# A two-layer hybrid decoder on one core: the first latent pair's rotary turn and key product move behind five steps of the next query projection

## The chip, the cores and the metric

One core of one Trainium2 chip runs the whole program in one launch. The metric is the device time of one execution in microseconds (us). PE is TensorE, with its weight loads apart (PEld); DVE is VectorE, ACT is ScalarE, POOL is GpSimd, SP is SyncE, whose queue issues the DMAs.

## The reference, cut to what matters

512 tokens of width 1024 go through two layers. Each begins with a mixer of three groups of heads: six latent heads (MLA) with a decoupled rotary key, six differential heads, four block-sparse heads (MoBA). Then come a cross-attention and an MLP.

```python
proj = n @ w_in                        # c_q 256, c_kv 128, k_r 32, dq dk dv 384 each, mq mk mv 256 each
qh  = to_heads(rmsnorm(c_q, q_norm) @ w_uq, 64 + 32)
kvh = to_heads(rmsnorm(c_kv, kv_norm) @ w_ukv, 64 + 64)
q_a = concatenate([qh[..., :64], apply_rope(qh[..., 64:], pos)])
k_a = concatenate([kvh[..., :64], broadcast(apply_rope(k_r, pos))])   # one rotary key for all six heads
o_a = causal_attention(q_a, k_a, kvh[..., 64:])
lam = exp(sum(lq1 * lk1)) - exp(sum(lq2 * lk2)) + lam_init
o_b = rmsnorm(diff_attention(dq, dk, dv, lam), sub_norm) * (1 - lam_init)
o_c = moba_attention(mq, mk, mv)
h = h + concatenate([o_a, o_b, o_c]) @ w_out
```

The output is the (1, 512, 1024) float32 trunk after both layers and a final norm.

## The kernel before, in words

**Precision.** Every float32 operand is kept as two parts, a high part (cast on ACT) and the rest (a subtraction on DVE or POOL), side by side in one tile. A product is three matmuls, high by high, high by low, low by high (`mm3`). `split` (L135, its casts L139, its subtractions L141) makes the two parts of an activation; for the kinds in `pool_kinds` ("mq", "kr", "q", "cq", "lat") the subtraction is on POOL, else on DVE. `halve` (L153) does the same for a weight block: ACT L156, then L161, in the mixer on POOL for the even blocks or as `vector_full` sets it. The subtraction of a score operand must end before the scores that read it.

**Work of the mixer** (L751). Eight pairs of heads, m0 to m2 (latent), d0 to d2 (differential), o0 and o1 (MoBA), have two kinds of work. *Units* (`head_units`): for one head and one block of 128 queries the scores on PE (128 to 512 columns), the mask and maximum on DVE (L637), the exponential on ACT (L639), the reciprocal and scaling on DVE (L707, L708; the second block's scaling on POOL), two units later the transposes of the probabilities (L279, evictions L671, L672), and per head a product with the values (`mix`). *Steps* (`Filler`, L55): the projections that make the pairs' queries, keys and values, in the order `fill_order` (L1434): kv, cq, tok, m0, d0, m1, d1, o0, m2, d2, o1, mem, cross. A 128x512 projection is eight steps (`proj_steps`, L288), each with three matmuls of 128x512 (a *step* below), one tick, and at its first and fifth step a weight block of 128x512. `weights` (L196) fetches two blocks ahead of the one that it hands out, so a step issues a load on SP's queue (L150, from `w_in` or `w_mla`) and its halving too.

The pipeline (L728) starts a unit, then draws steps worth `fill_time` from the filler, then finishes an older unit. The steps are thus what PE does while a unit's softmax is under way; their number in a layer is fixed. Before a pair's first unit, `drain` (L75) runs all steps up to that pair. `after(n, call)` (L307) hangs a call on a count of ticks (`tick`, L311). Matmuls of `mm3` are emitted with `hold=False`: the scheduler may move them, so the order on PE isn't quite that of the code.

**Around the change.** `tok` projects d0's and d1's values and the 32 columns of the rotary key. Its eviction is followed by `rotate` (L828): six small DVE operations (L834 to L836) turn the key by the positions' angles, a copy (L837) doubles it. `rotate` hangs `turn` (L840) on `chain_k` ticks: four transposes on PE into a "t" bank (L279), a copy on ACT (L846), a split of kind "kr" (ACT, then POOL, 64x512) into the first of four key tiles, and three DMAs on SP (L852) that copy it into the others. `mla_steps` for m0 makes the values of the pair (twelve matmuls of 128x128), the two queries (two 128x512 products of six matmuls, each multiplied by the rotary table, L889, and split on ACT and POOL, kind "mq"), then at L895 waits for the keys by ticking, and makes the key product (three matmuls of 128x512, L897 to L900), which is split on ACT and DVE into the lower halves of two key tiles. The scores of m0's first head need its query, the first key tile's both halves and nothing else. In layer 0 the lambda of the differential heads is computed beside the first units: a load (L475) and eight small DVE operations (L480, L481), then L487 and L488.

PSUM banks: three "mm" (projections), three "s" (scores, `mix`), two "t" (transposes).

Of the kernel before, what the change touches and what calls it, by code (L numbers as in the profile page):

```python
# [48 lines left out]
class Filler:  # L49
# [17 lines left out]
    def run(self, time):  # L67

        busy = False
        while self.todo and self.todo[0][2] in self.over and time > 0:  # L70
            time -= self.step()
            busy = True
        return busy
# [27 lines left out]
class Trunk:  # L101
# [649 lines left out]
    def mixer(self, l):  # L751
# [4 lines left out]
        fill = Filler()  # L756
# [101 lines left out]
            self.cq = yield from latent_steps([a["w_in"][l, 1], a["w_in"][l, 2]],  # L858
                                              self.gains["g_q"][:, 2 * l:2 * l + 2], 256)

        def mla_steps(p, got):
            def ready(there):
                while not there():
                    self.tick()

            ready(lambda: None not in self.ckv)
            (ckv,), cq = self.ckv, self.cq
            ws = [self.weights(a["w_mla"][l, p, :, :4 * P]), self.weights(a["w_mla"][l, p, :, 4 * P:])]

            def wb(j):  # L870
                js = slice(j % 4 * P, (j % 4 + 1) * P)
                return ws[j // 4][:, 0, js], ws[j // 4][:, 1, js]


            ps = self.psum("mm" if p else "t")
            for i in range(NQ):
                isl = slice(i * P, (i + 1) * P)
                self.mm3(ps[:, isl], (ckv[:, 0, isl], ckv[:, 1, isl]), wb(5), True, True)
            got["v"] = self.evict_values(ps)
            self.tick(2)  # L880
            yield 1300
            ready(lambda: None not in cq)
            got["q"] = []
            for e in range(2):
                ps = self.psum("mm")
                for j in range(2):
                    self.mm3(ps, wb(2 * e + j), (cq[j][:, 0, :], cq[j][:, 1, :]), j == 0, j == 1)
                t = self.tmp()
                nc.vector.tensor_tensor(t, ps, self.tab_q, ALU.mult)  # L889
                q = self.pair("B")  # L890
                self.split(q[:, 0, :], q[:, 1, :], t, kind="mq")
                got["q"].append(q)
                self.tick(2)
                yield 1280
            ready(lambda: self.keys)  # L895

            ps = self.psum("mm")  # L897
            self.mm3(ps, wb(4), (ckv[:, 0, :], ckv[:, 1, :]), True, True)
            got["k"] = self.keys[2 * (p % 2):2 * (p % 2) + 2]
            for e, k in enumerate(got["k"]):  # L900
                self.split(k[0:64, 0, :], k[0:64, 1, :], ps[64 * e:64 * e + 64, :])
            self.tick()
            yield 640

        def mla_units(p, got):
            units = []
            oo = {}

            def o():
                if "o" not in oo:  # L910
                    oo["o"] = self.tmp()
                return oo["o"]

            def done():
                outs[p] = self.finish_pair(o())

            for e in range(2):
                def terms(e=e):
                    q, k = got["q"][e], got["k"][e]
                    return [(q[:, i, :], k[:, j, :]) for i, j in ((0, 0), (0, 1), (1, 0))]  # L920

                units += self.head_units([terms], lambda i: self.causal[:, S - (i + 1) * P:], 1.0,
                                         lambda: got["v"], e, o, None, done if e else None)
            return units
# [28 lines left out]
        def pair_steps(p, got):  # L953

            at = 3 + 2 * p if p < 2 else 1 + 3 * p
            if p < 3:
                yield from qk_steps(at, got, "q", p, 2, (0, 0, 1))
                yield from qk_steps(at + 1, got, "k", None, 2, (0, 1, 0))
            else:
                yield from qk_steps(at, got, "q", p, 1, (0, 1))  # L960
                yield from qk_steps(at + 1, got, "k", None, 1, (0, 0), (1, 1))
            if p < 2:
                return

            ps = yield from self.proj_steps(a["w_in"][l, at + 2], x)

            def evict():
                t = self.tmp()
                nc.vector.tensor_tensor(t, ps, self.hnorm.rows, ALU.mult)
                self.after(3, lambda: turn(t))  # L970

            def turn(t):
                vt = self.psum("t")
                for i in range(NQ):
                    self.transpose(vt[:, i * P:(i + 1) * P], t[:, i * P:(i + 1) * P])
                got["v"] = self.evict_values(vt)

            self.hnorm.then(evict)
# [78 lines left out]

        got = {n: {"moves": []} for n in "d0 d1 d2 m0 m1 m2 o0 o1".split()}
        self.keys = []
        steps = {"kv": kv_steps, "cq": cq_steps, "tok": token_steps}  # L1060
        steps["mem"] = lambda: self.memory_steps(l)
        steps["cross"] = lambda: self.cross_memory_steps(l)
        units = {}
        for p in range(3):
            steps[f"d{p}"] = lambda p=p: pair_steps(p, got[f"d{p}"])
            steps[f"m{p}"] = lambda p=p: mla_steps(p, got[f"m{p}"])
            units[f"d{p}"], units[f"m{p}"] = pair_units(p, got[f"d{p}"]), mla_units(p, got[f"m{p}"])
        for p in range(2):
            steps[f"o{p}"] = lambda p=p: pair_steps(3 + p, got[f"o{p}"])
            units[f"o{p}"] = pair_units(3 + p, got[f"o{p}"])  # L1070
        for n in self.fill_order.split():
            fill.add(n, steps[n](), "m0" if n == "m2" else None)
        seq = []
        order = self.fill_order.split()
        for n in self.unit_order.split():
# [352 lines left out]
    def run(self):  # L1428
        nc = self.nc
        self.bufs = {"A": 8, "B": 21, "tmp": 11, "small": 40, "raw": 4, "w": 5, "pt": 2}  # L1430
        self.pbufs = {"mm": 3, "s": 3, "t": 2}
        self.ptags = {"o": "s"}

        self.fill_order = "kv cq tok m0 d0 m1 d1 o0 m2 d2 o1 mem cross"  # L1434
        self.unit_order = "m0 d0 m1 d1 o0 m2 d2 o1"
        self.fill_time = {1: 1870, 2: 1700}
        self.cross_fill_time = 4000
        self.mem_time = 300

        self.skew, self.tail_skew = 2, 2  # L1440

        self.wait_n, self.wait_l, self.wait_d = 8, 3, 3
        self.pow_d = 3
        self.chain_n, self.chain_l, self.chain_d, self.chain_k = 6, 12, 4, 2

        self.pool_kinds = ("mq", "kr", "q", "cq", "lat")
        self.vector_full = self.vector_all = False

        self.look, self.mlp_look = 2, 6
        self.plan = self.planned()  # L1450
        self.blocks = sum(1 for _ in self.planned())
        self.fetched = 2
        self.setup()
        g = self.gains
        self.sum_squares_start()
        self.hn = [self.norm_input(k, g["g_attn"][:, :KT], squares=False) for k in range(KT)]
        for k in range(KT):
            self.after(2 + k, lambda k=k: self.sum_squares_add(self.h[k], True))
        self.hnorm = Later()
        self.after(10, lambda: self.norm_of(self.hnorm, self.sq, NQ, 2))  # L1460
        self.setup_gains()
        self.after(12, self.setup_rotary)
        for n, part in enumerate(self.setup_distances()):
            self.after(24 + 2 * n, part)
        self.after(58, self.setup_lambda)
        self.memory_norm(34, 8)
        for l in range(L):
            gs = slice(l * KT, (l + 1) * KT)
            self.vector_full = True
            outs = self.mixer(l)  # L1470
            self.vector_full = False
            self.output(self.a["w_out"][l], outs, g["g_cross"][:, gs], (3, 0, 4, 1, 5, 2, 6, 7))
            outs = self.cross(l)
            parts = {n: [] for n in ("11", "21", "22", "t1", "t2", "t3", "t4", "y")}
            self.vector_all = True
            self.output(self.a["w_co"][l], outs, g["g_mlp"][:, gs], halves=parts)
            self.mlp(l, g["g_attn"][:, (l + 1) * KT:(l + 2) * KT] if l + 1 < L else None, parts)
            self.vector_all, self.look = False, 2
# [101 lines left out]
```

## Time and profile before

| | us |
|---|---|
| median of three runs | 1527.31 |
| the three runs | 1530.01, 1527.31, 1525.93 |
| the profiled execution, its own time | 1524.68 |
| its span | 1522.6 |
| PE busy | 1478.7 (97%) |
| DVE busy | 1048.5 (69%) |
| ACT busy | 854.1 (56%) |
| POOL busy | 362.9 (24%) |

The span is that of the instructions in the trace; the rest of the execution's time lies around them. The trace's mean TensorE clock is 0.995 of full speed. The times below are from the start of the span: layer 0's mixer has its units from about 62 to 274 us, layer 1's from about 812 to 1017 us.

### The profile page before, as it was taken

To read this page: it belongs to the slowest core of one execution; us is meant where nothing else is said; L and a number is where in the kernel's file an instruction comes from. 1 tells how busy PE (TensorE), PEld (TensorE's weight loads), DVE (VectorE), ACT (ScalarE), POOL (GpSimd) and SP (SyncE) were. 2 spreads that over 40 slices of the span, in tenths; PEclk is the share of its full clock that TensorE was granted. 3 is DMA by queue.
4 is the path that set the end of the run, shared out by engine and by line. 5 is a ranking of instruction groups with operands and counts; after the bars stand their busy time and mean duration, and the time that the engine had idled before them with its cause. 6 is when DMAs were issued, how large, how long until landed. Compare 5 with 4: busy or idle time off the path is not lost.

```text
span 1522.6 us, 24399 instructions
## 1 busy us (share of the span) xinstructions
PE 1478.7 (97%) x8648; PEld 1293.8 (85%) x8648; DVE 1048.5 (69%) x2316; ACT 854.1 (56%) x1823; POOL 362.9 (24%) x302
## 2 busy tenths in 40 slices
PE   7899999999999999999999999999999999999997
PEld 6778897888899899998887888888888989899887
DVE  7687887536699666676437788873378976677653
ACT  5576777535566544454446677764366654445441
POOL 2645374441000000000146446644400000000001
PEclk9999999999999999999999999999999999999999
DMA  4445543221223323223224535423202332333331
GB/s 154 125 107 140 153 133 110 81 93 49 88 72 125 108 92 100 98 103 97 97 75 122 154 101 158 114 90 96 98 30 76 110 120 92 103 98 103 111 98 56
DMA packets 90136, 157.22 MB, mean 103 GB/s; under 512 B 12064, under 2 KB 17056, under 8 KB 90016
## 3 DMA queue, kind: packets, MB, share of 16 engines
q1 hardware_dynamic: 89728, 155.63, 33.3%
q8 instruction: 68, 1.11, 0.3%
q14 instruction: 52, 0.43, 0.1%
q10 hardware_dynamic: 288, 0.05, 0.0%
HBM read 136.24 MB, written 2.10 MB: 91 GB/s over the span
## 4 chain that ended last, share of the span: by engine, by line
PE 74%; DVE 11%; ACT 5%; DMA 4%; issue 3%; POOL 2%; SPq 1%; POOLq 0%; DVEq 0%; ACTq 0%
PE mm L276 60%; PE s L276 11%; PE t L279 2%; DMA raw<-w 2%; ACT tmp L639 2%; DVE tmp L637 2%; DVE pt L672 1%; DVE tmp L712 1%; POOL w L161 1%; DVE tmp L260 1%; DVE B L141 1%; PE t L276 1%; ACT w L156 1%; DVE tmp L688 1%; DMA raw<-w_in 1%
## 5 line engine op out<-in xcount | busy, mean ns | idle before, releaser
L276 PE MATMUL mm<-B,w 128*128 128x512 f32 (+1 forms) x2490 | 574.3, 386 | 1.5 <-POOL B L141 1.4
L276 PEld LDWEIGHTS mm<-B,w 128*128 128x128 f32 x2490 | 453.2, 189 | 94.8 <-POOL B L141 2.8
L276 PE MATMUL mm<-A,w 128*128 128x512 f32 (+1 forms) x1920 | 384.7, 350 | 6.3 <-ACT A L143 5.9
L156 ACT CAST w<-raw 128x512 fp32r<-128x512 f32 (+1 forms) x372 | 224.7, 607 | 269.4 <-PE mm L276 209.0
L276 PEld LDWEIGHTS mm<-A,w 128*128 128x128 f32 x1920 | 310.1, 189 | 50.3 <-ACT A L143 5.9
L161 POOL TENSOR_TENSOR w<-raw,w 128x512 fp32r<-128x512 f32 (+2 forms) x180 | 226.7, 1267 | 218.9 <-ACT w L156 170.5
L409 POOL TENSOR_TENSOR tmp<-tmp,tmp 128x512 f32<-128x512 f32 (+1 forms) x25 | 30.1, 1206 | 655.3 <-ACT tmp L406 653.2
L161 DVE TENSOR_TENSOR w<-raw,w 128x512 fp32r<-128x512 f32 x192 | 134.7, 702 | 35.0 <-ACT w L156 34.7
L639 ACT ACTIVATE tmp<-tmp,small 128x384 f32<-128x384 f32 (+3 forms) x176 | 98.8, 562 | 60.2 <-DVE small L637 59.9
L1092 DVE TENSOR_TENSOR h<-mm,h 128x512 f32<-128x512 f32 x92 | 63.2, 687 | 67.9 <-PE mm L276 67.6
L276 PE MATMUL mm<-pt,B 128*128 128x256 f32 x768 | 102.9, 283 | 2.3 <-ACT tmp L1331 2.3
L139 ACT CAST B<-tmp 128x512 fp32r<-128x512 f32 (+2 forms) x156 | 91.9, 590 | 23.2 <-DVE tmp L688 5.9
L276 PEld LDWEIGHTS mm<-pt,B 128*128 128x128 f32 x768 | 95.8, 189 | 3.5 <-ACT tmp L1331 3.5
L260 DVE TENSOR_TENSOR tmp<-raw,raw 128x512 f32<-128x512 f32 x64 | 43.9, 686 | 66.1 <-DMA raw<-w 65.9
L263 ACT CAST B<-tmp 128x512 fp32r<-128x512 f32 x96 | 59.5, 620 | 51.2 <-DVE tmp L260 51.2
L279 PE MATMUL t<-ident,tmp 128*128 128x128 f32 (+1 forms) x444 | 75.0, 275 | 8.5 <-DVE tmp L837 3.2
L141 DVE TENSOR_TENSOR B<-tmp,B 128x512 fp32r<-128x512 f32 (+1 forms) x110 | 74.9, 681 | 12.1 <-ACT B L139 8.6
L279 PEld LDWEIGHTS t<-ident,tmp 128*128 128x128 f32 (+1 forms) x444 | 54.7, 141 | 24.2 <-issue 4.2
L141 POOL TENSOR_TENSOR B<-tmp,B 128x512 fp32r<-128x512 f32 (+1 forms) x46 | 61.9, 1353 | 48.2 <-ACT B L139 48.2
L276 PE MATMUL s<-pt,B 128*128 128x512 f32 (+3 forms) x352 | 71.3, 345 | 0.0
L338 POOL TENSOR_TENSOR small<-small,mhalf 128x4 f32<-128x4 f32 (+2 forms) x19 | 23.4, 1230 | 199.3 <-DVE small L372 174.5
L276 PE MATMUL mm<-w,A 128*128 128x512 f32 (+1 forms) x288 | 65.2, 365 | 3.6 <-DVE B L144 2.9
(195 smaller groups left out, 2115.1 us busy)
## 6 DMA issues: line engine op xcount, KB each, us to landing
raw<-w SPq DMA_DIRECT2D x256, 256.0 KB, 2.8
raw<-w_in SPq DMA_DIRECT2D x64, 256.0 KB, 3.2
st<-B SPq DMA_DIRECT2D x144, 64.0 KB, 2.0
raw<-w_ck SPq DMA_DIRECT2D x32, 256.0 KB, 3.0
raw<-w_cv SPq DMA_DIRECT2D x32, 256.0 KB, 2.7
raw<-w_out SPq DMA_DIRECT2D x32, 256.0 KB, 2.7
raw<-w_cq SPq DMA_DIRECT2D x32, 256.0 KB, 2.7
raw<-w_co SPq DMA_DIRECT2D x32, 256.0 KB, 2.6
```

The source lines that it names most:

```text
L139: nc.scalar.copy(hi, x)
L141: eng.tensor_tensor(lo, x, hi.bitcast(F32), ALU.subtract)
L156: self.nc.scalar.copy(w[:, 0, :], raw)
L161: eng.tensor_tensor(w[:, 1, :], raw, w[:, 0, :].bitcast(F32), ALU.subtract)
L260: nc.vector.tensor_tensor(got[name], x, y, op)
L263: nc.scalar.copy(w[:, 0, :], raw)
L276: self.in_order(self.nc.tensor.matmul(out, lhs, rhs, start=start, stop=stop, skip_group_check=open), hold)
L279: self.in_order(self.nc.tensor.transpose(out, x, self.ident))
L409: eng.tensor_tensor(s[:, :n], s[:, :n], self.sq[:, :n], ALU.add)
L637: nc.vector.tensor_tensor_reduce(out=t[:, :n], in0=s[:, :n], in1=bias, scale=-slope, scalar=TOP, op0=ALU.add, op1=ALU.min, accum_out=st[:, ...
L639: nc.scalar.activation(t[:, :n], t[:, :n], AF.Exp, bias=st[:, 0:1], scale=-1.0, accum_out=sums)
L1092: nc.vector.tensor_tensor(self.h[m], ps, self.h[m], ALU.add)
```

## The change

`chain_k` goes from 2 ticks to 11: the two of m0's values, two for each of its two queries, and five steps of the next entry of the fill order, d0, whose query projection is its first work. At L895 the loop that only ticked now draws steps of d0 until the rotary key is there. So in each layer the turn, its split and its DMAs, and m0's key product come after five of the eight steps of d0's query projection, which had come behind them. Those 15 matmuls are no longer there for the units later; the number of matmuls is the same.

```diff
-        def mla_steps(p, got):
+        def mla_steps(p, got, work):
...
-            ready(lambda: self.keys)
+
+            while not self.keys:
+                yield next(work["d0"])
...
+        work = {}
...
-            steps[f"m{p}"] = lambda p=p: mla_steps(p, got[f"m{p}"])
+            steps[f"m{p}"] = lambda p=p: mla_steps(p, got[f"m{p}"], work)
...
         for n in self.fill_order.split():
-            fill.add(n, steps[n](), "m0" if n == "m2" else None)
+            work[n] = steps[n]()
+            fill.add(n, work[n], "m0" if n == "m2" else None)
...
-        self.chain_n, self.chain_l, self.chain_d, self.chain_k = 6, 12, 4, 2
+        self.chain_n, self.chain_l, self.chain_d, self.chain_k = 6, 12, 4, 11
```

Lines of the changed kernel are two to four higher behind these places (L1156 becomes L1160, L932 becomes L934).

**PE, layer 0, from m0's last query product to its first scores**, before. `t_690` is the bank of the turn, `mm_730` m0's key product, `mm_750` d0's query projection, `s_740` the first scores.

```order
L279 MATMUL t_690<-ident,tmp_635 64x128 x4
L276 MATMUL mm_730<-B_572,w_613 128x512 x3
L276 MATMUL mm_750<-A_123,w_666 128x512 x3
L276 MATMUL mm_750<-A_126,w_666 128x512 x3
L276 MATMUL mm_750<-A_129,w_666 128x512 x3
L276 MATMUL mm_750<-A_132,w_666 128x512 x3
L276 MATMUL mm_750<-A_135,w_671 128x512 x3
L276 MATMUL mm_750<-A_138,w_671 128x512 x3
L276 MATMUL mm_750<-A_141,w_671 128x512 x3
L276 MATMUL mm_750<-A_144,w_671 128x512
L276 MATMUL s_740<-B_697,B_715 128x128 x3
```

The same place of the change (`t_745`, `mm_761`, `mm_714`, `s_771`):

```order
L276 MATMUL mm_714<-A_123,w_666 128x512 x3
L276 MATMUL mm_714<-A_126,w_666 128x512 x3
L276 MATMUL mm_714<-A_129,w_666 128x512 x3
L276 MATMUL mm_714<-A_132,w_666 128x512 x3
L276 MATMUL mm_714<-A_135,w_671 128x512 x3
L279 MATMUL t_745<-ident,tmp_635 64x128 x4
L276 MATMUL mm_761<-B_572,w_613 128x512 x3
L276 MATMUL mm_714<-A_138,w_671 128x512 x3
L276 MATMUL mm_714<-A_141,w_671 128x512 x2
L276 MATMUL s_771<-B_752,B_699 128x128
L276 MATMUL mm_714<-A_141,w_671 128x512
L276 MATMUL mm_714<-A_144,w_671 128x512 x2
```

Five steps stand ahead of the turn; of the eight, three are left behind the key product, partly between the first scores. Layer 1 reads the same.

**POOL, layer 0, the same place**, before. L161 halves a weight block, L141 of 128x512 is a query of m0, of 64x512 the rotary key.

```order
L161 TENSOR_TENSOR w_753<-raw_751,w_753 128x512
L161 TENSOR_TENSOR w_787<-raw_785,w_787 128x512
L141 TENSOR_TENSOR B_697<-tmp_695,B_697 64x512
L161 TENSOR_TENSOR w_824<-raw_822,w_824 128x512
L161 TENSOR_TENSOR w_905<-raw_903,w_905 128x256
L141 TENSOR_TENSOR B_715<-tmp_713,B_715 128x512
L141 TENSOR_TENSOR B_727<-tmp_725,B_727 128x512
```

And now:

```order
L161 TENSOR_TENSOR w_717<-raw_715,w_717 128x512
L161 TENSOR_TENSOR w_739<-raw_737,w_739 128x512
L141 TENSOR_TENSOR B_699<-tmp_697,B_699 128x512
L141 TENSOR_TENSOR B_711<-tmp_709,B_711 128x512
L161 TENSOR_TENSOR w_812<-raw_810,w_812 128x512
L141 TENSOR_TENSOR B_752<-tmp_750,B_752 64x512
L161 TENSOR_TENSOR w_871<-raw_869,w_871 128x256
```

The rotary key's split was ahead of the two queries' splits and comes behind both, and behind the next weight block (`w_812`), four operations of POOL in a row.

**DVE, layer 0, in m0's first units**, before. L480 and L481 are lambda's, `mm_750` is d0's query projection.

```order
L934 SCALAR_TENSOR_TENSOR tmp_814<-mm_750,qscale,rows_383 128x512
L672 TENSOR_TENSOR pt_857<-t_858,pt_857 128x128
L707 RECIPROCAL small_797<-small_796 128x1
L708 TENSOR_SCALAR tmp_802<-tmp_802,small_797 128x384
L672 TENSOR_TENSOR pt_857<-t_886,pt_857 128x256
L480 TENSOR_TENSOR small_832<-tmp_830 128x32
```

And now, from the last of lambda's eight small operations (`mm_809` is d0's key projection, `small_855` the third block's sum):

```order
L481 TENSOR_REDUCE small_821<-small_820 128x1
L637 ISA tmp_860,small_861<-s_856,causal 128x384
L637 ISA small_861 128x1
L487 TENSOR_TENSOR neg_lam<-small_822 128x1 x2
L488 TENSOR_SCALAR neg_lam<-neg_lam 128x1 x2
L707 RECIPROCAL small_855<-small_854 128x1
L637 ISA tmp_894,small_895<-s_890,causal 128x512
L637 ISA small_895 128x1
L708 TENSOR_SCALAR tmp_860<-tmp_860,small_855 128x384
L934 TENSOR_TENSOR tmp_906<-mm_809,rows_383 128x512
```

The eviction of d0's key projection (`tmp_906`) has come behind lambda's operations and the third block's scaling; the bank of `mm_809` is the one that PE needs for the second query product of m1.

## Rows read from the trace of the kernel before

**Rows 1.** The page, part 1: busy us (share of span), instructions.

```profile
PE 1478.7 (97%) x8648; PEld 1293.8 (85%) x8648; DVE 1048.5 (69%) x2316; ACT 854.1 (56%) x1823; POOL 362.9 (24%) x302
```

**Rows 2.** The waits of PE: engine, tile, line, releaser: us total, times, longest.

```profile
PE s L276 <- DVE tmp L688: 3.2, 6, 0.7
PE t L279 <- DVE tmp L837: 3.2, 2, 2.4
...
PE t L279 <- DVE tmp L708: 2.6, 1, 2.6
...
PE t L279 <- POOL tmp L708: 1.1, 1, 1.1
...
PE s L276 <- POOL B L141: 0.4, 2, 0.2
```

**Rows 3.** Timeline, PE, layer 0: start us, duration us, what, xcount [idle before, releaser].

```profile
53.30 2.12 PE L276 MATMUL mm<-B,w 128*128 128x512 f32 x8 [0.29 <-POOL B L141]
56.15 0.63 PE L279 MATMUL t<-ident,tmp 128*64 128x128 f32 x4 [0.73 <-DVE tmp L837]
...
57.31 5.17 PE L276 MATMUL mm<-A,w 128*128 128x512 f32 x22
62.33 0.33 PE L276 MATMUL s<-B,B 128*128 128x128 f32 x2
62.86 1.26 PE L276 MATMUL s<-B,B 128*128 128x128 f32 x7 [0.20 <-POOL B L141]
```

**Rows 4.** Timeline, PE, layer 1, the same place.

```profile
801.67 2.11 PE L276 MATMUL mm<-B,w 128*128 128x512 f32 x8 [0.28 <-POOL B L141]
806.22 0.63 PE L279 MATMUL t<-ident,tmp 128*64 128x128 f32 x4 [2.44 <-DVE tmp L837]
...
812.92 1.26 PE L276 MATMUL s<-B,B 128*128 128x128 f32 x7 [0.17 <-POOL B L141]
```

**Rows 5.** Timeline, POOL, layer 0, then layer 1.

```profile
56.20 1.29 POOL L161 TENSOR_TENSOR w<-raw,w 128x512 fp32r<-128x512 f32 x1 [1.70 <-ACT w L156]
...
808.25 1.29 POOL L141 TENSOR_TENSOR B<-tmp,B 64x512 fp32r<-64x512 f32 x1 [2.43 <-ACT B L139]
```

**Rows 6.** Timeline, DVE, layer 0, then layer 1: rotation, copy, query times table.

```profile
52.00 1.32 DVE L835 TENSOR_TENSOR tmp<-tmp,nsin 128x64 f32<-128x64 f32 x1
...
54.63 0.21 DVE L835 TENSOR_TENSOR tmp<-tmp,sin 128x64 f32<-128x64 f32 x1
...
805.93 0.23 DVE L837 COPY tmp<-tmp 128x128 f32<-128x128 f32 x1
806.08 1.28 DVE L889 TENSOR_TENSOR tmp<-mm,tab_q 128x512 f32<-128x512 f32 x2
```

**Rows 7.** Timeline, ACT, layer 0: the rotary key's first half.

```profile
57.43 0.62 ACT L139 CAST B<-tmp 64x512 fp32r<-64x512 f32 x1
```

**Rows 8.** Timeline, PE, layer 0 from 73 us, then layer 1.

```profile
73.35 1.45 PE L276 MATMUL mm<-w,B 128*128 128x128 f32 x12
77.38 0.63 PE L279 MATMUL t<-ident,tmp 128*128 128x128 f32 x4 [2.58 <-DVE tmp L708]
...
78.37 4.50 PE L276 MATMUL mm<-B,w 128*128 128x512 f32 x12
...
824.35 2.92 PE L276 MATMUL mm<-B,w 128*128 128x512 f32 x12
```

**Rows 9.** Windows, PE: us, PE busy (matmuls), granted clock, DMA share, GB/s.

```profile
78.00:81.00 3.00, 3.00 (x11) 0.56 0.23 53
...
807.00:809.00 2.00, 2.00 (x10) 1.00 0.33 110
```

**Rows 10.** Timeline, SP queue and DVE, layer 0: lambda's load and first product.

```profile
61.46 7.22 SPq L150 DMA_DIRECT2D raw<-w_in  x4
68.72 0.42 SPq L475 DMA_DIRECT2D tmp<-lam  x1
...
72.16 0.19 DVE L480 TENSOR_TENSOR small<-tmp 128x32 f32<-128x32 f32 x1 [1.50 <-DMA tmp<-lam]
```

## The prediction, made before the changed kernel ran

> **What bounds the kernel now.** I read the busy shares first, then the waits of PE, then the two places of the change in the timelines. PE is busy 1478.7 us, 97% of the span [rows 1], so what it idles, 43.9 us (the span of 1522.6 less that), is all that a change of order can win, and most of that isn't in reach. The waits [rows 2] show what is near the change: the turn's transposes wait for DVE's copy (L837) 3.2 us in two places, one in each layer; the first scores for POOL's split (L141) 0.4 us in two places; and in m0's units transposes wait once for POOL's scaling, 1.1 us, and once for DVE's scaling, 2.6 us. The last row of them, six waits of scores for DVE of 0.7 us at most, lies at the ends of the mixers.
>
> PE's timeline gives each its place. In layer 0 the last query product ends at 53.30 + 2.12 = 55.42, the turn waits 0.73 us, turn and key product take 56.15 to 57.31, and after the projection the scores wait 0.20 [rows 3]. In layer 1 the same waits are 2.44 and 0.17 [rows 4]. One matmul of 128x512 takes (62.33 - 57.31) / 22 = 0.228 us [rows 3]; this is the unit of all cover below.
>
> **What the profiled time is.** The sum is made against the profiled execution, 1524.68 us with 2.1 us outside its span; the median of the runs shown is 2.6 above it, and I put the sum on the median.
>
> **The change, part by part.** No matmul is added or taken away, and each moved step has its loads and halvings with it. Five steps, 15 matmuls or 3.4 us, go ahead of the turn in both layers, so there the copy is no longer waited for. What is late next is the rotary key's split on POOL. It now stands behind both queries' splits and one weight block; before, it stood ahead of them. PE sees it in the first scores.
>
> *Layer 1.* PE: 801.67 + 2.11 + 3.42 (five steps) + 1.16 (turn and key product) + 1.14 (five more matmuls ahead of the scores) = 809.50. POOL: the first query's product with its table can take the copy's place on DVE at 805.93 and lasts 0.64, half of 1.28 [rows 6]; its cast takes 0.62 [rows 7]; then come four operations of 1.29 each [rows 5], so the key is split at 805.93 + 0.64 + 0.62 + 5.16 = 812.35. Here the first score matmul needs only the key's high part, and it and three projection matmuls (0.8) fit in between. The new idle is 812.35 - 809.50 - 0.8 = 2.05, for 2.44 + 0.17 = 2.61 before [rows 4]: **-0.6**. Ends: -2.6 if POOL isn't late, +0.2 if nothing fits in between.
>
> *Layer 0.* PE is at the scores at 55.42 + 3.42 + 1.16 + 1.14 = 61.14. POOL is free of the weight block before at 56.20 + 1.29 = 57.49 [rows 5], and the same four operations end at 62.65. The first score matmul waits for the split here. Idle 1.5, for 0.73 + 0.20 before [rows 3]: **+0.6**. Ends: -0.9 and +1.2. The upper end is one more hold-up between DVE and POOL: the small rotation on DVE took 1.32 us where POOL worked beside it and 0.21 where not [rows 6], and an addition of two tiles on DVE (L1160) now stands beside those four operations.
> The Trainium skill, SBUF — State Buffer, section Who interferes with whom, says that a DVE instruction with two inputs in SBUF contends with a GpSimd instruction that reads SBUF, and whichever is first holds the port to its end. The two rotations agree, 1.32 against 0.21. By that rule the split would be later by up to an addition's length, about 0.65, and the sum 0.65 less negative; which engine is first there no row shows, so I leave it in the upper end.
>
> *Layer 0, m0's units.* The 1.1 us for POOL's scaling and the 2.6 us for DVE's [rows 2] are there because DVE's chain waits 1.50 us for lambda's load [rows 10]. After the second of these idles the clock is granted at 0.56 [rows 9], about half of 2.4 GHz, and 12 matmuls take 4.50 us for 2.92 in layer 1 [rows 8], 1.6 more. That is 5.3 in all, and it is this arrangement that the change breaks up. The key moves on SP come later, and two of the weight loads that stood behind them are ahead; lambda's load stood behind four loads in 7.22 us [rows 10], and so goes 2 x 1.8 = 3.6 earlier, at 65.1. It lands 72.16 - 68.72 = 3.4 later, at 68.5. Then DVE is no longer held by it but by the first block's transposes: 62.65, 22 matmuls (5.0), score products (about 1.4), transpose and evictions (about 0.75) give 69.8. From lambda to the scaling that PE waited for the chain took 77.38 - 72.16 = 5.2 [rows 8, 10], now to 75.0; and the eviction of d0's key projection, which now comes behind it, ends 0.64 later, 75.65. PE reaches the product that needs this bank at 62.65 + 11.7 = 74.35 (before, from 62.86 to 73.35 + 1.45 less the idle of 1.1 it had 10.8 of work; eight matmuls of 0.228 come in, a score product and two groups of transposes, some 0.9, go out). Idle 1.3, and 0.64 for one more eviction that the next bank waits for: 2.0 for 5.3. **-3.3**. That is under the 2.44 after which layer 1 kept its full clock [rows 4, 9], so I count no lost clock. Ends: -5.3 (no wait) and +0.6 (lambda lands as late as before; worked out below).
>
> *The ends of the mixers.* The steps moved ahead are missing later. By the order, PE has 71 projection matmuls between the transposes of the last three heads before and 58 now, in both layers: 13 x 0.228 = 3.0 us less cover, where DVE already makes PE wait 0.6 to 0.7 at a time [rows 2]. Output-projection matmuls fill in part. I take one to two more such waits, 1.0 a layer: **+2.0**. Ends: 0 and 2 x 15 x 0.228 = +6.8.
>
> *The middle units, the SP queue, the other keys.* Waits there are regrouped, none over 1.5: 0, ends -2 and +2. The three key moves are issued about 5 us later, but the first score that reads a copied key comes some 9 us after the first scores; if that cover went, it would be one landing, a case I give no share.
>
> Sum: -0.6 + 0.6 - 3.3 + 2.0 = **-1.3**, so 1523.4 against the profiled 1524.68 and 1526.0 on the median.
>
> **Rivals.**
> A, *the stalls just go*: POOL has time enough, lambda's and the bank's waits vanish, the ends have cover to spare. -2.6 - 0.9 - 5.3 = -8.8, 1518.5. For it: each of these waits lies next to a matmul that could fill it, and PE is the only bound. Against it: POOL's four operations in a row are longer than PE's work beside them in both layers.
>
> B, *the cover runs out at the ends, slower*: the last heads lack the moved matmuls one for one. +6.8 in place of +2.0 gives a sum of +3.5, 1530.8, and with one fall of the clock like that of [rows 8], 1.6, 1532.4. It decides once the ends cost more than the 3.3 that the rest gives back. For it: the number of steps is fixed, and these heads wait for DVE already. Against: 0.7 at most in each such wait, with no lost clock.
>
> C, *lambda's load comes no earlier*: SP is held by the key moves or the weight buffers. Then the chain ends at 77.38 + 0.64 = 78.0, PE idles 3.65 there, 0.64 behind it, and loses the clock's 1.6: 5.9 for 5.3. The sum is +2.6, 1529.9. For it: SP issues in order, and the moves still wait for POOL, later than before. Against: two of the four loads do stand ahead now.
>
> That the change doesn't do what it says is out: the five steps stand ahead of the turn in the order of both layers.
>
> **How the numbers follow.** 0.3% is 4.6 us, about what a measurement of this kernel can tell from no change. My forecast has 0.50, A 0.23, B 0.14, C 0.13. Faster (below 1522.7) is A and 0.04 of the forecast, 0.27; slower (above 1531.9) is 0.12 of B and 0.01 of C, 0.13; between them 0.60. The range goes from 1520.0, which takes in much of the way to A, to 1531.5, which takes in C and the lower half of B; about 0.1 is left out at either end.
>
> **What would show it.** Right: no wait of the transposes for L837 in either layer; scores that wait for POOL's L141 about 1.5 and 2.0 us; a wait of a projection for DVE's L934 near 75 us, and full clock behind it; lambda's first product no longer waiting for its load; at most 1 us more idle a layer at 255 to 274 and at 998 to 1017. Wrong: the POOL wait under 0.5 in both (A), DVE still waiting for lambda past 71 us (C), several waits on L688 of 1 us and more at the ends (B).

## The result, and the profile after

The change made the kernel slower: 1551.65 us in the median of four runs (1549.22 to 1558.66) against 1526.62 (1525.0 to 1530.01), a ratio of 1.0168 with a 95% interval of 1.0141 to 1.0194. That is 25 us, where the forecast was no change and the range ended at 1531.5.

The profiled execution took 1558.66, 7 above its median; its span is 1556.9. Of that, 2.2 us lie ahead of anything that the change moves: m0's last query product ends at 57.67 us for 55.42 [rows 3]. The page, part 1:

```profile
PE 1500.9 (96%) x8648; PEld 1306.6 (84%) x8648; DVE 1065.0 (68%) x2316; ACT 853.6 (55%) x1823; POOL 359.6 (23%) x302
```

No matmul was added, yet PE is busy 22.2 us longer than in [rows 1]; it idles 56.0 us (1556.9 less 1500.9), 12.1 more than before. So a third of the 34 us of span is idle time, and two thirds are the same matmuls taking longer. Most of these two thirds is the clock: its mean is 0.984 here and 0.995 before, 1.6% of the one span and 0.5% of the other, which makes some 17 us (an estimate). That share belongs to this execution. The other three of the changed kernel have a mean clock of 0.989 to 0.991, and by the same working 6 to 9 us are clock, of the 25 to 28 by which their spans are longer than that of before. The waits of PE (columns as in [rows 2]; a line behind the change has a number two higher, so L1036 is L1034 of before):

```profile
PE t L279 <- DVE tmp L1036: 6.6, 2, 3.5
...
PE t L276 <- ACT tmp L1024: 4.1, 3, 1.9
...
PE mm L276 <- DVE tmp L934: 3.1, 1, 3.1
...
PE mm L276 <- ACT w L156: 2.6, 1, 2.6
...
PE mm L276 <- POOL w L161: 2.3, 5, 0.6
...
PE s L276 <- POOL B L141: 1.8, 2, 1.0
...
PE s L276 <- DVE tmp L688: 1.0, 3, 0.4
```

The waits that the prediction began with are gone: no transpose waits for L837, nor for L708, and the waits for L688 are 1.0 us where they were 3.2 [rows 2]. What came is new: L1036 and L1024, the norm chain of a differential pair (squares on ACT, column sums on PE, a chain of small operations on DVE, transposes on PE); L156 and L161, weights that aren't halved in time; L934, the eviction of d0's key projection. PE at the place of the change, layer 0 and then layer 1:

```profile
53.22 4.45 PE L276 MATMUL mm<-B,w 128*128 128x512 f32 x11 [0.86 <-POOL B L141]
...
60.92 0.60 PE L279 MATMUL t<-ident,tmp 128*64 128x128 f32 x4
...
65.33 0.44 PE L276 MATMUL s<-B,B 128*128 128x128 f32 x2 [0.81 <-POOL B L141]
...
79.64 2.00 PE L276 MATMUL mm<-B,w 128*128 128x512 f32 x6 [3.12 <-DVE tmp L934]
...
825.57 0.33 PE L276 MATMUL s<-B,B 128*128 128x128 f32 x1 [0.85 <-ACT B L139]
...
827.65 0.44 PE L276 MATMUL s<-B,B 128*128 128x128 f32 x2 [1.01 <-POOL B L141]
```

The query product ends at 53.22 + 4.45, the turn (60.92) waits for nothing. The scores wait for POOL's split 0.81 us in layer 0; in layer 1 the first of them waits 0.85 for the key's cast on ACT (L139), the next 1.01 for POOL. The product behind the bank waits 3.12. These are the waits of [rows 3, 4, 8] in their new form. The larger ones lie far behind the change. In layer 1:

```profile
889.50 0.33 PE L276 MATMUL mm<-w,B 128*128 128x128 f32 x1 [2.59 <-ACT w L156]
...
890.50 2.61 PE L276 MATMUL mm<-w,B 128*128 128x128 f32 x11 [0.19 <-POOL w L161]
...
955.61 1.05 PE L276 MATMUL t<-halves,tmp 128*128 128x2 f32 x8 [1.89 <-ACT tmp L1024]
...
968.40 1.12 PE L279 MATMUL t<-ident,tmp 128*128 128x128 f32 x4 [3.04 <-DVE tmp L1036]
```

Behind three of these idles the windows (columns as in [rows 9]) show the clock granted at half or little more:

```profile
80.00:84.00 4.00, 4.00 (x15) 0.60 0.31 73
892.00:896.00 4.00, 4.00 (x17) 0.50 0.57 184
968.00:972.00 4.00, 3.60 (x15) 0.57 0.30 103
```

It fell behind shorter idles too. In layer 0 the transposes of the column sums wait 1.34 us for L1024 at 192.02, and then

```profile
194.00:196.00 2.00, 2.00 (x11) 0.50 0.96 308
```

and behind the 0.85 and 1.01 of layer 1's first scores it is 0.57 from 828 to 832 us, with 1.00 in the 4 us before.

Where it accumulates can be read from the end of each head's product with the values, counted from the end of m0's last query product (worked out from the timelines of PE):

| us from the end of m0's last query product | layer 0 before | after | layer 1 before | after |
|---|---|---|---|---|
| d0, first head | 57.2 | 60.7 | 53.1 | 57.8 |
| d0, second head | 69.8 | 77.4 | 65.7 | 80.4 |
| d1, second head | 124.1 | 130.1 | 119.2 | 131.8 |
| o0, first head | 138.7 | 151.9 | 133.7 | 153.4 |
| o1, second head (the last) | 218.4 | 231.8 | 213.3 | 232.7 |

Until d0's first head the difference is 3.5 and 4.7, most of it the 3.4 us of steps that now come first. Then there are two jumps in each layer: in d0's second head (4 and 10 us) and in the first head behind d1 (7 in both). Of the first, some 1.5 us are work and no loss: m1's values, twelve matmuls of 128x128 (1.45 us in [rows 8]), come into this head with the shift, and until d1's second head the difference falls again by 1.6 and 2.1. From o0's first head on it stays about as it is, though the 3.4 us of steps that came first are then missing behind. The three places are called **P1** (m0's first head), **P2** (d0's second head) and **P3** (behind d1) in the expectations.

### The profile page after: what moved, and what is told of

Same layout as the page of the kernel before. It is cut to its first block, busy times and chain, and to the rows that moved or that the text cites. A ratio compares the mean times of both kernels' runs of the same rounds, so it can differ in the third digit from the quotient of the medians.

```text
span 1556.9 us, 24408 instructions
## 1 busy us (share of the span) xinstructions
PE 1500.9 (96%) x8648; PEld 1306.6 (84%) x8648; DVE 1065.0 (68%) x2316; ACT 853.6 (55%) x1823; POOL 359.6 (23%) x302
## 4 chain that ended last, share of the span: by engine, by line
PE 74%; DVE 11%; ACT 6%; issue 3%; DMA 3%; POOL 2%; SPq 0%; POOLq 0%; DVEq 0%; ACTq 0%
PE mm L276 60%; PE s L276 11%; PE t L279 2%; ACT tmp L639 2%; DVE tmp L637 1%; DMA raw<-w 1%; POOL w L161 1%; DVE B L141 1%; DVE tmp L712 1%; ACT w L156 1%; ACT B L139 1%; DVE pt L672 1%; PE t L276 1%; DVE tmp L688 1%; DVE tmp L260 1%
## 5 line engine op out<-in xcount | busy, mean ns | idle before, releaser
L276 PE MATMUL mm<-A,w 128*128 128x512 f32 (+1 forms) x1920 | 392.6, 354 | 8.6 <-ACT A L143 6.0
L156 ACT CAST w<-raw 128x512 fp32r<-128x512 f32 (+1 forms) x372 | 224.6, 606 | 273.7 <-PE mm L276 207.9
L276 PEld LDWEIGHTS mm<-A,w 128*128 128x128 f32 x1920 | 314.7, 192 | 55.3 <-ACT A L143 6.0
L161 POOL TENSOR_TENSOR w<-raw,w 128x512 fp32r<-128x512 f32 (+2 forms) x180 | 224.6, 1256 | 247.9 <-ACT w L156 205.9
L161 DVE TENSOR_TENSOR w<-raw,w 128x512 fp32r<-128x512 f32 x192 | 133.6, 696 | 34.9 <-ACT w L156 34.7
L139 ACT CAST B<-tmp 128x512 fp32r<-128x512 f32 (+1 forms) x156 | 92.2, 592 | 20.7 <-DVE tmp L688 7.0
L141 DVE TENSOR_TENSOR B<-tmp,B 128x512 fp32r<-128x512 f32 (+1 forms) x110 | 82.5, 750 | 11.6 <-ACT B L139 7.6
L279 PE MATMUL t<-ident,tmp 128*128 128x128 f32 (+1 forms) x444 | 78.7, 286 | 8.8 <-DVE tmp L1036 6.6
L141 POOL TENSOR_TENSOR B<-tmp,B 128x512 fp32r<-128x512 f32 (+1 forms) x46 | 61.0, 1332 | 76.0 <-ACT B L139 48.0
L279 PEld LDWEIGHTS t<-ident,tmp 128*128 128x128 f32 (+1 forms) x444 | 57.2, 147 | 24.9 <-DVE tmp L1036 7.0
L671 ACT CAST pt<-t 128x128 fp32r<-128x128 f32 (+3 forms) x128 | 53.3, 418 | 26.0 <-PE t L279 25.5
L276 PEld LDWEIGHTS s<-pt,B 128*128 128x128 f32 x352 | 59.7, 193 | 8.8 <-ACT pt L671 1.8
```

The costliest lines, as they stand in the source:

```text
L139: nc.scalar.copy(hi, x)
L141: eng.tensor_tensor(lo, x, hi.bitcast(F32), ALU.subtract)
L156: self.nc.scalar.copy(w[:, 0, :], raw)
L161: eng.tensor_tensor(w[:, 1, :], raw, w[:, 0, :].bitcast(F32), ALU.subtract)
L276: self.in_order(self.nc.tensor.matmul(out, lhs, rhs, start=start, stop=stop, skip_group_check=open), hold)
L279: self.in_order(self.nc.tensor.transpose(out, x, self.ident))
```

## The experiments

**Which half of the change costs.** The theory S: the steps drawn ahead shift the whole later sequence of steps against the units, and the loads, halvings and chains there meet in another way. The rivals: T, the late turn and key split cost by themselves; E, the ends of the mixers lack cover. The first kernel keeps the late turn and lets the steps be owed.

```diff
             while not self.keys:
+                fill.owed += 1
                 yield next(work["d0"])
...
     def run(self, time):
         busy = False
+        if self.owed:
+            self.owed -= 1
+            time -= 640
```

> The change, but the five steps drawn ahead are owed: each of the first five units of m0 draws one step less, so that from m0's sixth unit on every engine's order is that of the kernel before; the turn stays behind five steps. Theory S (the later work is shifted against the units by five steps, and that costs): the loss of 25 us goes, 1522 to 1530, and no wait of 1.5 us or more on PE is left behind m0. Rival T (the late turn and the late key split cost by themselves, the rest follows from them): still 1545 or more. Rival E (the ends of the mixers lack cover): also back at 1522 to 1530, told from S by where the idle time of the change lies.

Measured 1525.7 us, ratio 0.9996 (0.9986 to 1.0006): the loss is gone. Its waits near the change, in the waits of PE (all lines four higher):

```profile
PE s L280 <- DVE small L641: 4.5, 4, 2.7
...
PE s L280 <- POOL B L145: 1.7, 2, 1.1
```

The late turn is there with its waits for POOL, 1.7 us in all, and one new wait of scores for L637 (here L641) of 2.7 us in m0's units, in the place of those for L708. So what the prediction spent most of its steps on is worth nothing either way, and T falls as the main cause. The second kernel is the other half.

```diff
-        self.chain_n, self.chain_l, self.chain_d, self.chain_k = 6, 12, 4, 11
+        self.chain_n, self.chain_l, self.chain_d, self.chain_k = 6, 12, 4, 2
...
             self.tick()
             yield 640
+            for _ in range(5 if p == 0 else 0):
+                yield next(work["d0"])
```

> Only the shift: the rotary turn comes as early as before (2 ticks), and five steps of d0's query projection are drawn behind m0's key product, ahead of the first unit. From the first scores on the order is that of the change. S: 1545 to 1556, the loss is all here, with the waits for L1036 and L1024 as in the change. T: 1525 to 1532. E: 1545 to 1556, with the idle time in the last three heads.

Measured 1546.66, ratio 1.0136 (1.0115 to 1.0156): 20 of the 25 us come with the steps alone. Whether the 5 that are left belong to the late turn is within what the two intervals leave open.

**By layer.** In `rotate`, for layer 0 as here, and for layer 1 in the same way.

```diff
-                self.after(self.chain_k, lambda: turn(t))
+                self.after(self.chain_k if l == 0 else 2, lambda: turn(t))
```

> The change in layer 0 alone (chain_k 11 there, 2 in layer 1). S: about half of the 25 us, 1535 to 1543, and layer 1 as before. T: the loss lies where the turn was late, about half here too. If the loss were a chance fall of the clock somewhere else, 1525 to 1530.

> The change in layer 1 alone. S: the other half, 1535 to 1543; the two single layers' losses add up to that of the change within 4 us. If one layer's loss carries over to the other: the sum misses by more.

Measured 1537.55 (ratio 1.0078, 1.0049 to 1.0107) and 1540.43 (1.0095, 1.0073 to 1.0117), so +11.1 and +14.0 against 1526.44 in the same runs, together 25.1. The layers add up, and the loss is in both. The jump at P2 isn't a chance of one execution: with the change in layer 1 alone it is 9.8 us there, 10.0 in the change.

**By place.** The same debt, paid in d1's units, leaves P1 and P2 and takes P3 away; steps drawn ahead only from d1's units on leave P3 alone.

```diff
+                    def start(n=n, need=need, start=start):
+                        fill.drain(need)
+                        fill.pay = fill.pay or n == "d1"
+                        start()
...
+        if self.owed and self.pay:
+            self.owed -= 1
+            time -= 640
```

> The change, but the five steps are owed in d1's first five units: the order is that of the change through m0, d0 and m1, and to within a step that of the kernel before from d1's second head on. The change is put at three places: P1, m0's first head (1.5 to 2 us a layer); P2, d0's second head, where PE waits for late weights behind the moves on SP's queue (4 to 10 a layer); P3, the first head behind d1, where d1's norm chain meets the loads and halvings of the cross-attention's keys (6 to 7 a layer). If so, P1 and P2 stay and P3 goes: 1536 to 1544. If the loss came from too little work at the mixers' ends: 1524 to 1530.

Measured 1546.48, ratio 1.0134 (1.0117 to 1.0151): +21.7 on 1524.76 in the same runs, above the range expected. E's figure is far off. In the profiled execution the jump at P3 is gone: from d1's second head to o0's first it is 15.0 us in both layers, for 14.6 and 14.5 before and 21.8 and 21.6 in the change. The jumps at P2 are still there, 4.0 and 9.6. Some 5 us more of its loss lie behind o0's first head, at neither place; the expectation didn't have them, and their cause stays open. The other kernel has the turn early again (`chain_k` 2) and this instead:

```diff
+                        if n == "d1":
+                            fill.extra = 5
...
+        if self.extra:
+            self.extra -= 1
+            time += 640
```

> The turn early and m0, d0 and m1 as in the kernel before; d1's first five units each draw one step more, so that only from there on the work is ahead as in the change. P3 alone: 1534 to 1542, with the waits for L1036 of about 3 us and half clock behind them in both layers, and none for the weights in d0. If P3 needs what P2 left behind: 1525 to 1530.

Measured 1536.31, ratio 1.007 (1.0055 to 1.0085): +11.5, P3 alone, as expected. By the ratios the two sum to 31 us, with an interval of some 3.5 either way, for 26 in the change, with one of 4: whether the places add up stays open. P3's mark stands in the waits of PE (L1040 and L841 here are L1036 and L837 of the change), beside the old wait for the turn:

```profile
PE t L283 <- DVE tmp L1040: 7.3, 2, 3.6
...
PE t L283 <- DVE tmp L841: 3.3, 2, 2.4
```

**What P3 is made of.** In the change, DVE's timeline in layer 1 up to the wait for L1036, and POOL's beside it:

```profile
962.45 1.40 DVE L708 TENSOR_SCALAR tmp<-tmp,small 128x384 f32<-128x384 f32 x1
963.76 1.25 DVE L342 SCALAR_TENSOR_TENSOR small<-small 128x8 f32<-128x8 f32 x1
964.94 0.28 DVE L672 TENSOR_TENSOR pt<-t,pt 128x128 fp32r<-128x128 f32 x1
965.14 1.10 DVE L343 TENSOR_TENSOR small<-small,small 128x8 f32<-128x8 f32 x1
966.28 1.19 DVE L344 SCALAR_TENSOR_TENSOR small<-small,small 128x8 f32<-128x8 f32 x1
```

```profile
962.33 5.12 POOL L161 TENSOR_TENSOR w<-raw,w 128x512 fp32r<-128x512 f32 x4 [1.56 <-issue]
```

Before, the three small operations of the chain (128x8) were:

```profile
929.23 0.15 DVE L342 SCALAR_TENSOR_TENSOR small<-small 128x8 f32<-128x8 f32 x1
...
930.92 0.16 DVE L344 SCALAR_TENSOR_TENSOR small<-small,small 128x8 f32<-128x8 f32 x1
```

They took 0.15 to 0.16 us; now 1.10 to 1.25, and a scaling that takes 0.41 in most places 1.40, while POOL halves four blocks of `w_ck` without a gap. The eviction L672 in their midst, which reads PSUM and SBUF, took 0.28 as ever. The products of the cross-attention's keys come, with the shift, some 7 us earlier against d1's end, and the halvings of their weights fall into d1's norm chain. These products began 10.0 us behind d1's product with the values in layer 0 of before (188.02 less 178.03 in PE's timeline) and 3.2 us behind it now (189.47 less 186.26). The test takes POOL out: `weights` passes `vector` for the blocks of `w_ck`. (In the mixer `vector_full` is set, and with it POOL halves every block, not the even ones alone.)

```diff
-    def halve(self, raw, tag="w"):
+    def halve(self, raw, tag="w", vector=False):
...
+        if vector:
+            eng = self.nc.vector
```

> The change with the weights of the cross-attention's keys (w_ck) halved on DVE, not on POOL. If the norm chain's small operations on DVE are slow at P3 because POOL halves weights beside them (1.1 to 1.25 us for 0.16), they take 0.2 here, the two waits for L1036 (3.5 and 3.0) fall under 1.5 and the time to 1540 to 1548. If the chain is late because the loads land late or the queue of DVE is long, the waits stay at 3 or grow, since DVE has 0.7 us more to do for each block: 1550 to 1558.

Measured 1540.78, ratio 1.0103 (1.0088 to 1.0118): by the ratios 10 of the 25 us come back. Of the 6.6 us of waits for L1036 0.2 are left, and the chain's operations in layer 1 (lines two higher) are as before:

```profile
950.74 0.16 DVE L344 SCALAR_TENSOR_TENSOR small<-small 128x8 f32<-128x8 f32 x1
...
952.03 0.15 DVE L346 SCALAR_TENSOR_TENSOR small<-small,small 128x8 f32<-128x8 f32 x1
```

The Trainium skill, SBUF — State Buffer, Who interferes with whom, says that a DVE instruction with two inputs in SBUF contends with a GpSimd instruction that reads SBUF, and that the one which is first holds the port to its end. The trace agrees, with 1.10 to 1.25 us for 0.16 beside halvings of 1.28, and with the eviction from PSUM that isn't held. The scaling L708, which has one tensor as its input, was held as well (1.40 for 0.41); of that the sentence says nothing.

**What P2 is made of.** SP's queue in layer 1, ahead of PE's wait of 2.59 at 889.50:

```profile
876.45 0.45 SPq L150 DMA_DIRECT2D raw<-w_mla  x1
881.44 3.67 SPq L624 DMA_DIRECT2D st<-B  x6
885.16 0.58 SPq L150 DMA_DIRECT2D raw<-w_mla  x1
```

The second block of m1's weights (`w_mla`) is issued at 885.16, 8.7 us after the first, behind six moves; the queue stood idle ahead of these from 876.9 to 881.4. What PE then waits for at 889.50 is the cast (L156) for m1's values, 128x128 products of these weights. The late load looks like the cause, but ACT's timeline doesn't end the wait there:

```profile
888.33 0.72 ACT L639 ACTIVATE tmp<-tmp,small 128x512 f32<-128x512 f32 x1 [2.20 <-DVE small L637]
...
889.05 0.39 ACT L156 CAST w<-raw 128x256 fp32r<-128x256 f32 x1
```

The load landed 2.4 us after its issue, at about 887.6. The cast stands in ACT's order behind an exponential, which waited for the maximum L637 (887.55 on DVE), and that stood behind the eviction of a product (L971, 886.94), which began as PE's last one ended (886.90). By the timelines this wait runs from PE's last product through DVE and ACT back to PE. In layer 0 the same head has no such wait, only two for POOL's halvings of 0.62 and 0.56. The test fetches one block further ahead in the mixers; the cast and the halving come a block earlier with the load.

```diff
+            self.look = 3
             outs = self.mixer(l)
+            self.look = 2
```

> The change with three weight blocks fetched ahead in the mixers, not two. If P2 is a weight load issued too late, behind key moves that wait on SP's queue, then PE's waits for L156 and L161 in d0's second head (2.6 and 0.6) shrink to nothing and the time falls to 1536 to 1546. If the loads are held by the bandwidth or by the buffers, the waits stay: 1549 to 1556.

Measured 1551.81, ratio 1.0174 (1.0154 to 1.0193): no gain, though the wait for L156 is gone from the list.

```profile
PE t L276 <- ACT tmp L1024: 9.3, 4, 3.2
...
PE t L279 <- DVE tmp L1036: 5.1, 2, 2.6
```

In layer 1 d0's second head took 15.4 us, for 22.6 in the change and 12.6 before, so P2 went there. Part of it was given back at P3, where the first head behind d1 took 23.4 us for 21.6: the column sums wait 9.3 us in all, 4.1 in the change. The rest can't be followed from one execution of each (this one lies 3.0 under its median, that of the change 7.0 above). The expectation that the time would follow the wait failed. Since load and cast come earlier together, the run doesn't tell which of the two made the wait; the timeline of ACT speaks for the cast's place. The next two kernels have the `w_ck` halvings on DVE and this, the second `look` 3 as well.

```diff
-                nc.scalar.activation(sq, ot, AF.Square)
+                nc.vector.tensor_tensor(sq, ot, ot, ALU.mult)
```

> The change with the w_ck halvings on DVE as in the run before, and the norm chain's squares on DVE too, not on ACT behind weight casts that wait for their loads. If ACT's queue is the rest of P3, the waits of the column sums (4.6 us in three places) go, and the clock falls that follow them: 1530 to 1537. If not: 1539 to 1543.

> The same with three weight blocks fetched ahead. With P3 out of the way, P2 can be won by the earlier loads, which in the run of that alone went over into longer waits for the squares: 1524 to 1531, little above the kernel before. If P2 isn't a matter of the loads: as the run before it.

Measured 1548.06 (ratio 1.0142, 1.0124 to 1.016) and 1547.39 (1.0122, 1.0097 to 1.0148): neither faster than the kernel with the halvings alone (1.0103), the first slower. The wait of PE in the first of them, and its ACT and DVE in layer 0 ahead of the squares:

```profile
PE t L278 <- DVE tmp L1026: 5.9, 4, 2.5
```

```profile
186.57 0.62 ACT L156 CAST w<-raw 128x512 fp32r<-128x512 f32 x1 [0.27 <-DMA raw<-w_ck]
187.22 0.58 ACT L689 COPY tmp<-s 64x512 f32<-64x512 f32 x1
```

```profile
187.87 0.68 DVE L163 TENSOR_TENSOR w<-raw,w 128x512 fp32r<-128x512 f32 x1
188.58 0.69 DVE L690 TENSOR_TENSOR tmp<-s,tmp 64x512 f32<-64x512 f32 x1
189.31 0.69 DVE L163 TENSOR_TENSOR w<-raw,w 128x512 fp32r<-128x512 f32 x1
189.92 0.68 DVE L1026 TENSOR_TENSOR tmp<-tmp 128x512 f32<-128x512 f32 x1
```

The column sums wait for the squares on DVE (L1026) as they did on ACT, 5.9 us in four places. The squares need a sum that takes in ACT's copy L689 (L687 of the change), and that copy still stands behind a cast of a w_ck block that waits for its load. So the move took one operation out of that queue and left the one ahead of it there. The cast and its wait are 0.9 us here, less than the 1.84 that PE waits at this place. The larger part is on DVE: two of the halvings (L163) that these kernels have there stand ahead of the sum L690 and ahead of the squares L1026, 1.4 us. What takes POOL's halvings out of the chain puts them into DVE's own order. The expectation failed. What the chain would take with ACT's casts out of its way too, and what part of the rest is P2's, stays open: no kernel with the shift takes all of it away.

**Fewer steps.** Three steps ahead of the turn.

```diff
-        self.chain_n, self.chain_l, self.chain_d, self.chain_k = 6, 12, 4, 11
+        self.chain_n, self.chain_l, self.chain_d, self.chain_k = 6, 12, 4, 9
```

> The change with three steps ahead of the turn, not five. If the loss comes from where the later loads and chains meet, it need not go with the number of steps: P3 is there when the w_ck blocks come within some 5 us of d1's last product, and by the counts of matmuls they are half as far ahead here; P2 may be gone. 1528 to 1540. If the loss went with the matmuls missing later, three fifths of 25: 1541 within 2.

Measured 1543.14, ratio 1.0107 (1.0093 to 1.0121): +16.4, close to three fifths of 25 (15; by the time alone that reading is not excluded) and above the first range. The waits of PE tell more than the time:

```profile
PE t L279 <- DVE tmp L1036: 11.4, 4, 4.1
...
PE t L279 <- DVE small L707: 3.0, 1, 3.0
```

The waits for L1036 are 11.4 us in four places, two in each layer, against 6.6 in two: with fewer steps ahead d0's chain runs into late operations as well as d1's. By its waits the loss isn't a share of the change's, but another one.

**A better kernel?** The debt paid in m0's units, and the rotary key's low part on DVE.

```diff
-        self.pool_kinds = ("mq", "kr", "q", "cq", "lat")
+        self.pool_kinds = ("mq", "q", "cq", "lat")
```

> The five steps owed in m0's units, as in the first run, and the rotary key's low part made on DVE and not behind the queries' splits on POOL. If POOL's order is what the first scores still wait for, the waits for L141 of 0.8 to 1.0 us a layer go and the time falls by 1 to 3 us, to 1521.5 to 1524.5, faster than both kernels. If DVE is as late, no change: 1524 to 1527.

Measured 1527.06, ratio 1.0 (0.9991 to 1.0008): no change. The waits for POOL went, and others stand there (lines four higher), the longest of them:

```profile
PE s L280 <- DVE small L641: 6.3, 5, 2.7
```

No version measured here beats the kernel before.

## Why the prediction was wrong, point by point

*What the change removes.* Right: the waits for L837 (3.2) and L708 (3.7 with POOL's) are gone. Measured with the shift taken back, in the first experiment, the late turn with all that hangs on it is worth -0.6 us, with an interval of -2.1 to +0.9.

*Layers 1 and 0, the key split on POOL.* Right in kind, over in size. In layer 1 the waits are 1.86 for a predicted 2.05, but 0.85 of it is for ACT's cast of the key, which the term didn't count as a wait of PE. In layer 0 it is 0.81 for 1.5: there too the first score matmul and three of the projection went ahead of the split, 0.8 that the term gave to layer 1 alone.

*m0's units, -3.3: too hopeful.* The wait for the bank came as forecast, at the place forecast, but was 3.12 for 1.3, and the clock fell behind it (0.60 in the windows above), so little of the 5.3 was won. This is the price of rival C (3.65 and a fall of the clock), but not its reason, since lambda's load did come earlier. SP's queue and DVE in layer 0:

```profile
68.56 1.26 SPq L475 DMA_DIRECT2D tmp<-lam  x1
```

```profile
73.40 0.27 DVE L480 TENSOR_TENSOR small<-tmp 128x32 f32<-128x32 f32 x1 [1.59 <-DMA tmp<-lam]
...
74.26 1.56 DVE L1160 TENSOR_TENSOR tmp<-tmp,tmp 128x512 f32<-128x512 f32 x1
...
78.90 0.68 DVE L934 TENSOR_TENSOR tmp<-mm,rows 128x512 f32<-128x512 f32 x1
```

Lambda's load was issued 10.9 us after m0's last query product (68.56 less 57.67), 13.3 before, so 2.4 earlier for 3.6; its first product came 4.8 us after the issue for 3.4; and the addition L1160 between lambda's operations took 1.56 us (0.68 as L1156 before). DVE was ready with the eviction 21.9 us after that product, for a predicted 20.2. The hold-up of DVE by POOL, which I left in the upper end of another term, was in this one.

*The ends of the mixers, +2.0: about right.* The last three heads take 25.1 us in both kernels in layer 0 (193.3 to 218.4 before, 206.7 to 231.8 after, from the origin of the table) and 25.0 in layer 1, though by the order 7 of the 128x512 matmuls fewer (6 in layer 1) stand there after the change: 1.4 to 1.6 us a layer that isn't won. Rival B put 3.4 a layer there. It forecast the side, not the mechanism: most of the loss is in place before these heads begin.

*The middle units, "0, ends -2 and +2": this is the step that failed.* I had counted 15 matmuls that come ahead as the same work in another place, and looked for its price at the place that it left and the one that it went to. But the filler is one sequence, and each of the steps behind these five comes five steps earlier against the units from there on. Most of the loss of 25 us is in this term: 20 with the shift alone, none with the shift taken back, 11.5 with P3 alone. How it is made is shown for part of it: 10 us went when POOL's halvings were taken out of the norm chain; the rest, P2 and what stays of P3, is located but not explained to the end. It was in reach of the views that I had: PE's order shows the products of the cross-attention's keys moved close behind d1's product with the values, and [rows 6] gave the price of such a meeting on DVE, 1.32 for 0.21.

*The clock.* I counted one fall of 1.6 us in a rival, and none in the forecast, since a wait of 2.44 had kept the full clock. That was one case taken for a rule: in the changed kernel the clock fell behind 1.34, and behind 0.85 and 1.01. By the mean clocks it makes some 17 of the 34 us of the profiled execution and 6 to 9 of 25 to 28 in the others (estimates, above). I had priced each new wait at its own length, and not what the clock loses behind it.

*The chances.* Slower had 0.13, on the ends (B) and on lambda's load (C), which make up little of the loss; nothing in the range stood for a shift of everything behind the change.

## What to carry to other kernels

Where one sequence of filler work feeds many consumers, a step drawn early moves all steps behind it, so its price is to be looked for at every place where loads, halvings and short serial chains meet, until the sequence is drained; or the debt is paid at once, as the first experiment did, and nothing behind it moves. A chain of tiny operations on DVE is worth keeping apart from POOL's long ones: each took nearly as long as one of POOL's here. And where PE is the bound, a wait is priced with the fall of the clock that may follow it, a short one too.

## What the runs showed of the hardware that was not expected

Operations of 128x8 on DVE took 1.10 to 1.25 us, seven times their 0.16, beside POOL's halvings of 1.28, and 0.16 again with the halvings elsewhere. Lambda's first product came 4.8 us after its load was issued, 3.4 before; the issue itself took 1.26 us on SP's queue for 0.42, and the rest isn't explained. The clock fell to half or little more behind PE's idles of 2.59, 3.04 and 3.12 us in the change and of 2.58 before [rows 8, 9], and also behind one of 1.34 and behind 0.85 and 1.01 together, but not behind one of 2.44 [rows 4, 9]: the length of one idle alone doesn't tell.
